# Three changes to a hybrid encoder block: weight splits moved between engines, left factors moved ahead, a projection's tile shape

## The chip, the cores and the metric

One core of a Trainium2 chip runs the whole layer. Its engines work side by side, each through its own queue in order: TensorE (PE; its weight loads are listed as PEld) multiplies, VectorE (DVE), ScalarE (ACT) and GpSimd (POOL) work element by element, SyncE (SP) issues the DMAs. The metric is the device time of one execution in microseconds. [...]

## The reference

One encoder layer on x of 512 x 1024 in float32, conditioned on a vector c:

```
mod = silu(c) @ w_ada + b_ada                     # sh1, sc1, g1, sh2, sc2, g2
u   = layer_norm(x) * (1 + sc1) + sh1
z   = u @ w_in                                    # q f i g u v ga gb, 1024 columns each
y_a = hgrn2_mixer(zq, zf, zi, zg) @ w_proj_a      # gated linear recurrence, chunks of 64
y_b = gmlp_mixer(zu, zv) @ w_proj_b               # gelu(u) * (W_s layer_norm(gelu(v)) + b)
mix = (sigmoid(zga + b0) * y_a + sigmoid(zgb + b1) * y_b) @ w_out
h   = layer_norm(alpha * x + g1 * mix) * ln1_w + ln1_b
u2  = layer_norm(h) * (1 + sc2) + sh2
a, b = split(u2 @ w_ffn_in);  ffn = (silu(a) * b) @ w_ffn_out
out = layer_norm(alpha * h + g2 * ffn) * ln2_w + ln2_b
```

## The kernel before, in words

Every float32 product is made of three fp32r matmuls: each operand is split into a rounded high part (ScalarE copies it to fp32r, L149 and L381) and the rest (a subtraction, mostly on VectorE, L150 and L382), and `mm3` (L216) adds high x high, high x low and low x high. So each block of weights, up to 1 MB, is loaded by SP into one of two `raw` buffers and split into one of two pairs `whi`, `wlo`, before TensorE may use it. `Block.split_part(k, n, eng)` (L138) splits n of a block's row groups, with the low part on the engine `eng`; `get()` (L203) hands out the next block and, one tick later, splits the block after it and loads the one after that. A tick is a mark in TensorE's order of work: `later(n, fn)` writes fn's instructions out n ticks on.

TensorE's and SP's order is that of the program. The other engines' order is made by a planner, which takes what it reckons ready, by program order or by a stated priority. Only in the lead stage (L423 to L511) are VectorE, ScalarE and GpSimd in the order written, too, and a few instructions elsewhere are pinned to it (`keep_in_program_order`, so the first two uq sums of `mixes`, L552).

The lead stage makes layer_norm(x) transposed and modulated (`uf`, split into `uh`, `ul`) one group k of 128 channels at a time, and multiplies it at once with the first 6 x 128 columns of `zu`, two k for each of four blocks of 256 x 768 weights (`lead`, 9 matmuls of 512 columns a half). The scale and shift of channels 2p, 2p+1 come from eight multiply-adds of VectorE over rows of w_ada (`step`, L342, 128x512) into `adaacc`, eight matmuls against ones (L361, the function `fin`), and an addition (L363). One turn p of the loop (L481) has in VectorE's order: steps 2 and 3 of the next pair of k, the low part `ul` of k+1, steps 4 to 7, then the additions after L361, steps 0 and 1 of the pair after, and `ul` of k+2. The next block's two row groups are split in the middle of the turn: high parts on ScalarE, low parts on GpSimd (L499, the engine `G`).

After it come the remaining two column groups of zu (`zw`, the plain columns, 48 matmuls), and then zv as a product in seven factors (`zt7`, L599: 24 matmuls each, with sums of weights for four of the factors, L191, and sums of left sides made by `mixes`, L542: four sums `uq` of high and low parts, four further sums and four splits, each 128x1024).

The output projection (w_out, scaled by `gate1` at L147 before its split) runs with tokens as the stationary side: `gemm_t` (L228) takes 128 tokens tt and one of four blocks of 1024 x 256 of w_out, 24 matmuls with 256 columns moving. The first block's products for tt 0 and 1 stand ahead (`head`, L1016). Each 128 x 512 half result is added to the residual (L1042) and put into statistics (L1043); then layer norm, a second one (`un`, L1030), a transposition on TensorE (L979), modulation and splits into `left` factors for the FFN's products (L1093), with weights `prod` split by L381 and L382.

Of the kernel before, what the change touches and what calls it, by code (L numbers as in the profile page):

```python
# [11 lines left out]
OP = mybir.AluOpType  # L12
# [38 lines left out]
def body(ctx, tc, x, c, w_ada, b_ada, w_in, b_gate, lb_logits, norm_w, w_proj_a, g_ln_w, g_ln_b,  # L51
# [52 lines left out]
    def tick():  # L104
        clock[0] += 1
        run_due()
# [109 lines left out]
    def mm3(ps, ah, al, bh, bl, start, stop):  # L216
        PE.matmul(ps, ah, bh, start=start, stop=False)  # L217
        PE.matmul(ps, ah, bl, start=False, stop=False)  # L218
        PE.matmul(ps, al, bh, start=False, stop=stop)  # L219
# [8 lines left out]
    def gemm_t(ps, w, tt, ah, al, k0=0, k1=KT):  # L228

        s = slice(tt * P, tt * P + P)  # L230
        for k in range(k0, k1):
            mm3(ps, ah[k][:, s], al[k][:, s], w[0][:, k, :], w[1][:, k, :], k == 0, k == KT - 1)
        if k1 == KT:
            tick()
# [19 lines left out]
    blocks += [Block([wcols(w_out, q * 256, 256)], gate=lambda q=q: gate1[:, q * 256:(q + 1) * 256], pool=(None if q == 1 else (lambda: (ub, ua)) if q == 3 else (lambda: (ub, ub)))) for q in range(4)]  # L254
# [168 lines left out]
    with tc.manual_schedule(engines={mybir.EngineType.DVE, mybir.EngineType.Activation, mybir.EngineType.Pool}):  # L423
# [57 lines left out]
        for p in range(KT // 2):  # L481
# [15 lines left out]
            if more:  # L497
                for kk in range(2):
                    nxt.split_part(kk, 1, G)  # L499
            else:  # L500
                nxt.split()
# [7 lines left out]
            if more:  # L509
                x_transpose(k + 3)  # L510
# [135 lines left out]

    zw(8 - NL, lambda j, ps: A.activation(gu[j], ps, AF.Gelu), j0=NL)
    later(5, gmlp_params)
    later(8, w_transpose)
    for fn in mixes(ua, True):  # L650
        fn()
# [364 lines left out]
    head = [acc_ps().rearrange("p (a b) -> p a b", a=2) for _ in range(2)]  # L1016
    for k in ((0, KT - 1), (KT - 1, KT)):
        for tt in range(2):
            gemm_t(head[tt][:, 0, :], wo[0], tt, mh, ml, *k)
# [12 lines left out]
    for tt in range(NT):  # L1032
        ht = h1t(tt)
        bst = sm.tile([P, 2, 6], F32, name="bst")
        for hf in range(2):
            first = hf == 0 and tt < 2
            ps = head[tt] if first else acc_ps().rearrange("p (a b) -> p a b", a=2)
            for i in range(first, 2):
                gemm_t(ps[:, i, :], wo[2 * hf + i], tt, mh, ml)
            with ahead_of_weights():  # L1040
                sl = slice(hf * 512, (hf + 1) * 512)
                V.scalar_tensor_tensor(ht[:, sl], ht[:, sl], ALPHA, ps.rearrange("p a b -> p (a b)"), op0=OP.mult, op1=OP.add)  # L1042
                V.bn_stats(bst[:, hf, :], ht[:, sl])  # L1043
# [241 lines left out]
```

## Time and profile before

| | us |
|---|---|
| median of three runs | 936.15 (934.73 to 936.59) |
| the profiled execution | 935.53 |
| its span, first to last instruction | 933.7 |
| TensorE busy | 899.9 (96%) |
| VectorE busy | 731.7 (78%) |
| ScalarE busy | 412.4 (44%) |
| GpSimd busy | 144.3 (15%) |
| mean granted clock | 0.993 |

Of 933.7 us TensorE is idle for 33.8. The page's slices show TensorE at nine tenths or more in nearly all of the 40 slices, so a gain can come from its idle time, or from doing its work in fewer or cheaper matmuls. A matmul's row gives its start and a modelled duration that overlaps the next one; the pace is the distance between starts. In a timeline, the bracket at the end of a row is the idle time of the engine just before it and what ended that.

### The profile page before, as it was taken

To read this page: it belongs to the slowest core of one execution; us is meant where nothing else is said; L and a number is where in the kernel's file an instruction comes from. 1 tells how busy PE (TensorE), PEld (TensorE's weight loads), DVE (VectorE), ACT (ScalarE), POOL (GpSimd) and SP (SyncE) were. 2 spreads that over 40 slices of the span, in tenths; PEclk is the share of its full clock that TensorE was granted. 3 is DMA by queue.
4 is the path that set the end of the run, shared out by engine and by line. 5 is a ranking of instruction groups with operands and counts; after the bars stand their busy time and mean duration, and the time that the engine had idled before them with its cause. 6 is when DMAs were issued, how large, how long until landed. Compare 5 with 4: busy or idle time off the path is not lost.

```text
span 933.7 us, 13131 instructions
## 1 busy us (share of the span) xinstructions
PE 899.9 (96%) x5357; PEld 794.2 (85%) x5357; DVE 731.7 (78%) x1036; ACT 412.4 (44%) x542; POOL 144.3 (15%) x99
## 2 busy tenths in 40 slices
PE   5899999999999999999999999999999999999995
PEld 4677778888788888888888999899999999888884
DVE  5858995897987788886389878987888888974337
ACT  4355543334466676764323327634444445531210
POOL 2310020200000000000000011006665544000001
PEclk9999999999999999999999999999999999999998
DMA  9844225442333331312297634022343221832312
GB/s 309 280 127 176 93 82 175 163 153 91 88 96 90 89 85 53 91 46 91 71 348 233 234 106 137 1 91 91 113 140 111 91 91 56 306 136 91 113 46 90
DMA packets 107822, 118.33 MB, mean 127 GB/s; under 512 B 3617, under 2 KB 89714, under 8 KB 107762
## 3 DMA queue, kind: packets, MB, share of 16 engines
q1 hardware_dynamic: 106592, 117.45, 39.0%
q8 instruction: 42, 0.69, 0.3%
q10 hardware_dynamic: 1170, 0.05, 0.1%
q14 instruction: 18, 0.15, 0.1%
HBM read 115.39 MB, written 2.10 MB: 126 GB/s over the span
## 4 chain that ended last, share of the span: by engine, by line
PE 81%; DVE 11%; DMA 2%; ACT 2%; issue 2%; POOL 1%; POOLq 0%; DVEq 0%; ACTq 0%; SPq 0%
PE acc L1093 15%; PE acc L219 15%; PE acc L217 15%; PE acc L218 15%; PE sps L1093 7%; PE acc L599 5%; DVE adaacc L342 2%; POOL rn L307 1%; PE sps L818 1%; PE sps L599 1%; DMA ada<-in_w_ada_dram 1%; DVE h L314 1%; PE sps L361 1%; PE sps L668 1%; PE sps L862 1%
## 5 line engine op out<-in xcount | busy, mean ns | idle before, releaser
L1093 PE MATMUL acc<-left,prod 128*128 128x256 f32 x1296 | 159.6, 283 | 0.4 <-DVE left L382 0.4
L1093 PEld LDWEIGHTS acc<-left,prod 128*128 128x128 f32 x1296 | 157.2, 192 | 0.6 <-DVE left L382 0.6
L149 ACT ACTIVATE whi<-raw 128x1024 fp32r<-128x1024 f32 (+2 forms) x92 | 90.7, 1016 | 136.9 <-PE acc L219 64.8
L150 DVE TENSOR_TENSOR wlo<-raw,whi 128x1024 fp32r<-128x1024 f32 (+2 forms) x85 | 99.9, 1191 | 45.2 <-ACT whi L149 39.9
L217 PE MATMUL acc<-uh,whi 128*128 128x512 f32 x336 | 134.7, 401 | 0.0
L219 PE MATMUL acc<-uh,wlo 128*128 128x512 f32 x336 | 131.4, 391 | 1.2 <-DVE wlo L150 1.2
L218 PE MATMUL acc<-ul,whi 128*128 128x512 f32 x336 | 131.0, 390 | 0.0
L219 PEld LDWEIGHTS acc<-uh,wlo 128*128 128x128 f32 x336 | 63.0, 188 | 15.2 <-DVE wlo L150 1.6
L1093 PE MATMUL sps<-left,prod 128*128 128x256 f32 x576 | 73.4, 283 | 2.0 <-DVE prod L382 2.0
L218 PEld LDWEIGHTS acc<-ul,whi 128*128 128x128 f32 x336 | 63.3, 188 | 12.0
L217 PEld LDWEIGHTS acc<-uh,whi 128*128 128x128 f32 x336 | 63.2, 188 | 11.7
L1093 PEld LDWEIGHTS sps<-left,prod 128*128 128x128 f32 x576 | 70.8, 192 | 2.4 <-DVE prod L382 2.4
L342 DVE SCALAR_TENSOR_TENSOR adaacc<-ada,cond,adaacc 128x512 f32<-128x512 f32 x82 | 70.4, 859 | 2.1 <-DMA ada<-in_w_ada_dram 0.6
L382 DVE TENSOR_TENSOR prod<-raw,prod 128x1024 fp32r<-128x1024 f32 x42 | 54.9, 1308 | 21.2 <-ACT prod L381 21.2
L307 POOL TENSOR_TENSOR rn<-rn,mhalf 128x1 f32<-128x1 f32 x16 | 18.5, 1158 | 339.6 <-DVE rn L306 339.6
L218 PE MATMUL acc<-wlo,hs 128*128 128x512 f32 x176 | 68.5, 389 | 0.0
L217 PE MATMUL acc<-whi,hs 128*128 128x512 f32 x176 | 68.5, 389 | 0.0
L219 PE MATMUL acc<-whi,hs 128*128 128x512 f32 x176 | 68.5, 389 | 0.0
L381 ACT ACTIVATE prod<-raw 128x1024 fp32r<-128x1024 f32 x42 | 44.4, 1058 | 41.2 <-PE acc L1093 21.4
L382 DVE TENSOR_TENSOR prod<-rawu,prod 128x1024 fp32r<-128x1024 f32 x22 | 47.7, 2169 | 8.3 <-ACT prod L381 7.8
L871 POOL TENSOR_TENSOR ss<-ss,mhalf 128x4 f32<-128x4 f32 x8 | 8.1, 1014 | 268.1 <-DVE ss L870 268.1
L217 PEld LDWEIGHTS acc<-whi,hs 128*128 128x128 f32 x176 | 33.0, 188 | 6.9
(293 smaller groups left out, 1854.0 us busy)
## 6 DMA issues: line engine op xcount, KB each, us to landing
ada<-in_w_ada_dram SPq DMA_DIRECT2D x32, 512.0 KB, 9.3
raw<-in_w_in_dram SPq DMA_DIRECT2D x13, 1024.0 KB, 5.7
raw<-in_w_in_dram SPq DMA_DIRECT2D x24, 512.0 KB, 5.4
raw<-in_w_ffn_in_dram SPq DMA_DIRECT2D x11, 1024.0 KB, 5.2
rawu<-in_w_ffn_in_dram SPq DMA_DIRECT2D x11, 1024.0 KB, 7.7
raw<-in_w_ffn_out_dram SPq DMA_DIRECT2D x10, 1024.0 KB, 5.1
ada<-in_w_ada_dram SPq DMA_DIRECT2D x8, 1024.0 KB, 7.8
rawq<-in_w_in_dram SPq DMA_DIRECT2D x4, 1024.0 KB, 7.9
```

The costliest lines, as they stand in the source:

```text
L149: A.activation(hi[:, k:k + n, :], self.raw[:, k:k + n, :], AF.Copy)
L150: eng.tensor_tensor(lo[:, k:k + n, :], self.raw[:, k:k + n, :], f32(hi[:, k:k + n, :]), OP.subtract)
L217: PE.matmul(ps, ah, bh, start=start, stop=False)
L218: PE.matmul(ps, ah, bl, start=False, stop=False)
L219: PE.matmul(ps, al, bh, start=False, stop=stop)
L307: G.tensor_tensor(rn[:, 0:1], rn[:, 0:1], mhalf[:, 0:1], OP.pow)
L314: V.scalar_tensor_tensor(xa, xa, rn[:, 0:1], wb[:, 1, :], op0=OP.mult, op1=OP.add)
L342: V.scalar_tensor_tensor(a, r, cond[:, k:k + 1], a, op0=OP.mult, op1=OP.add)
L381: A.activation(hi, src, AF.Copy)
L382: V.tensor_tensor(lo, src, f32(hi), OP.subtract)
L599: PE.matmul(o, a[:, k, s], b[:, k, :], start=n in (1, 5, 6) and k == 0 and a is ah and b is w[0], stop=n in (2, 4, 3) and k == 3 and a is ...
L1093: PE.matmul(ps[:, i, :], w[:, wi, k, cl], a[:, ai, k, :], start=first and st == (0, 0, 0, 0), stop=last and st == (1, 3, 0, 1), skip_group ...
```

## The change

The low part of the first row group of each next lead block is now made on VectorE behind steps 4 to 7, and the second row group is split at the end of the turn, behind `ul` of k+2, on VectorE too. `mixes(ua, True)` stands ahead of the plain columns. w_out is cut into four blocks of 512 x 512 in place of 1024 x 256 (rows q % 2, columns q // 2), `gemm_t` takes two of them for 24 matmuls with 512 columns moving, and ticks twice in it (before: once for each 24 matmuls of 256). `head` so makes the whole first half, 512 columns, for tt 0 and 1.

```diff
--- before.py
+++ after.py
@@ -229,9 +229,9 @@
 
         s = slice(tt * P, tt * P + P)
         for k in range(k0, k1):
-            mm3(ps, ah[k][:, s], al[k][:, s], w[0][:, k, :], w[1][:, k, :], k == 0, k == KT - 1)
-        if k1 == KT:
-            tick()
+            mm3(ps, ah[k][:, s], al[k][:, s], w[k // 4][0][:, k % 4, :], w[k // 4][1][:, k % 4, :], k == 0, k == KT - 1)
+            if k % 4 == 3:
+                tick()
 
     SEC = {n: i * D for i, n in enumerate(["q", "f", "i", "g", "u", "v", "ga", "gb"])}
     NL = 6
@@ -251,7 +251,9 @@
     blocks += [Block(fqg[2 * i:2 * i + 2]) for i in range(12)]
     blocks += [Block([wcols(w_in, SEC["ga"] + q * 256, 256)]) for q in range(4)]
     blocks += [Block([wcols(w_proj_a, q * 256, 256)]) for q in range(4)]
-    blocks += [Block([wcols(w_out, q * 256, 256)], gate=lambda q=q: gate1[:, q * 256:(q + 1) * 256], pool=(None if q == 1 else (lambda: (ub, ua)) if q == 3 else (lambda: (ub, ub)))) for q in range(4)]
+    blocks += [Block([w_out[q % 2 * 512:(q % 2 + 1) * 512, q // 2 * 512:(q // 2 + 1) * 512]], 4, 512,
+                     gate=lambda q=q: gate1[:, q // 2 * 512:(q // 2 + 1) * 512],
+                     pool=(None if q == 1 else (lambda: (ub, ua)) if q == 3 else (lambda: (ub, ub)))) for q in range(4)]
     KB = [(0, 4), (4, 4), (8, 4), (20, 2), (12, 4), (16, 4)]
 
 
@@ -495,8 +497,7 @@
             if more:
                 steps(p + 1, 4, 8)
             if more:
-                for kk in range(2):
-                    nxt.split_part(kk, 1, G)
+                nxt.split_part(0, 1)
             else:
                 nxt.split()
             lead(k + 1, w, 0)
@@ -507,6 +508,7 @@
                 modulate(k + 2)
             lead(k + 1, w, 1)
             if more:
+                nxt.split_part(1, 1)
                 x_transpose(k + 3)
         bpos[0] = KT // 2
     for j in range(NL):
@@ -644,11 +646,11 @@
             A.activation(gp["wT"][0:64, 4 * h:4 * h + 4, :], ps[0:64], AF.Copy)
             A.activation(gp["wT"][64:128, 4 * h:4 * h + 4, 64:128], ps[64:128, :, 64:128], AF.Copy)
 
+    for fn in mixes(ua, True):
+        fn()
     zw(8 - NL, lambda j, ps: A.activation(gu[j], ps, AF.Gelu), j0=NL)
     later(5, gmlp_params)
     later(8, w_transpose)
-    for fn in mixes(ua, True):
-        fn()
     gv = [ub.tile([P, 2, D], F32, name=f"gv{i}", tag="u") for i in range(2)]
     zt7(lambda tt: gv[tt // 2][:, tt % 2, :], AF.Gelu)
     for tt in (2, 3, 0, 1):
@@ -1013,10 +1015,10 @@
                 left_split(3, a12, ts)
 
 
-    head = [acc_ps().rearrange("p (a b) -> p a b", a=2) for _ in range(2)]
+    head = [acc_ps() for _ in range(2)]
     for k in ((0, KT - 1), (KT - 1, KT)):
         for tt in range(2):
-            gemm_t(head[tt][:, 0, :], wo[0], tt, mh, ml, *k)
+            gemm_t(head[tt], wo[0:2], tt, mh, ml, *k)
 
     mlag, nlag = [5, 5, 5, 9], [5, 5, 5, 3]
     rn2, uns = {}, {}
@@ -1034,12 +1036,12 @@
         bst = sm.tile([P, 2, 6], F32, name="bst")
         for hf in range(2):
             first = hf == 0 and tt < 2
-            ps = head[tt] if first else acc_ps().rearrange("p (a b) -> p a b", a=2)
-            for i in range(first, 2):
-                gemm_t(ps[:, i, :], wo[2 * hf + i], tt, mh, ml)
+            ps = head[tt] if first else acc_ps()
+            if not first:
+                gemm_t(ps, wo[2 * hf:2 * hf + 2], tt, mh, ml)
             with ahead_of_weights():
                 sl = slice(hf * 512, (hf + 1) * 512)
-                V.scalar_tensor_tensor(ht[:, sl], ht[:, sl], ALPHA, ps.rearrange("p a b -> p (a b)"), op0=OP.mult, op1=OP.add)
+                V.scalar_tensor_tensor(ht[:, sl], ht[:, sl], ALPHA, ps, op0=OP.mult, op1=OP.add)
                 V.bn_stats(bst[:, hf, :], ht[:, sl])
         with ahead_of_weights():
             mv, rn = ln_fin(bst)
```

## Rows read from the trace of the kernel before

**Rows 1.** Waits of TensorE, whole span: in total, times, the longest (us).

```profile
PE sps L361 <- DVE adaacc L342: 5.7, 3, 2.4
...
PE acc L599 <- DVE wlo L382: 2.1, 3, 1.6
PE sps L1093 <- DVE prod L382: 2.0, 2, 1.1
PE acc L219 <- DVE wlo L150: 1.2, 1, 1.2
PE sps L599 <- DVE wlo L382: 0.9, 1, 0.9
```

**Rows 2.** The chain that ended last, lead stage: start, us, what.

```profile
41.44 2.23 DVE adaacc L342
...
45.95 0.76 DVE adaacc L342
```

**Rows 3.** Timeline of GpSimd, lead stage: start, us, instruction, [idle before, releaser].

```profile
40.83 4.53 POOL L150 TENSOR_TENSOR wlo<-raw,whi 128x768 fp32r<-128x768 f32 x2 [8.21 <-ACT whi L149]
```

**Rows 4.** Timeline of VectorE, lead stage.

```profile
19.86 0.96 DVE L150 TENSOR_TENSOR wlo<-raw,whi 128x768 fp32r<-128x768 f32 x1 [0.54 <-ACT whi L149]
...
48.01 0.16 DVE L363 TENSOR_TENSOR mod<-sps,bmod 128x4 f32<-128x4 f32 x1 [1.31 <-PE sps L361]
...
49.69 0.69 DVE L412 TENSOR_TENSOR ul<-uf,uh 128x512 fp32r<-128x512 f32 x1 [0.32 <-ACT uh L411]
...
52.62 6.04 DVE L342 SCALAR_TENSOR_TENSOR adaacc<-ada,cond,adaacc 128x512 f32<-128x512 f32 x4
```

**Rows 5.** Timeline of ScalarE, lead stage.

```profile
39.92 1.56 ACT L149 ACTIVATE whi<-raw 128x768 fp32r<-128x768 f32 x2
```

**Rows 6.** Timeline of TensorE, lead stage.

```profile
33.32 1.44 PE L361 MATMUL sps<-ones,adaacc 128*128 128x128 f32 x8 [2.37 <-DVE adaacc L342]
...
46.85 1.13 PE L361 MATMUL sps<-ones,adaacc 128*128 128x128 f32 x8 [1.66 <-DVE adaacc L342]
...
58.80 1.13 PE L361 MATMUL sps<-ones,adaacc 128*128 128x128 f32 x8 [1.67 <-DVE adaacc L342]
...
70.49 0.39 PE L217 MATMUL acc<-uh,whi 128*128 128x512 f32 x1
```

**Rows 7.** Stretches: length, busy of PE PEld DVE ACT POOL (count), clock, DMA share, GB/s.

```profile
34.00:38.00 4.00, 4.00 (x15) 3.25 (x14) 2.82 (x6) 1.41 (x2) 0.00 (x0) 0.57 1.09 349
...
42.00:44.00 2.00, 2.00 (x10) 1.62 (x10) 1.97 (x2) 0.00 (x0) 2.00 (x2) 1.00 0.05 20
```

**Rows 8.** Timeline of VectorE from the plain columns to the third factor.

```profile
64.92 2.36 DVE L150 TENSOR_TENSOR wlo<-raw,whi 128x1024 fp32r<-128x1024 f32 x2 [0.26 <-ACT whi L149]
72.79 2.36 DVE L382 TENSOR_TENSOR wlo<-raw,whi 128x1024 fp32r<-128x1024 f32 x2 [5.51 <-ACT whi L381]
75.07 2.35 DVE L550 TENSOR_TENSOR uq<-uh,ul 128x1024 f32<-128x1024 f32 x2
...
90.04 1.22 DVE L382 TENSOR_TENSOR mix<-uq,mix 128x1024 fp32r<-128x1024 f32 x1
```

**Rows 9.** The chain, whole span: a run of 512-column matmuls, one of 256.

```profile
108.15 10.91 PE acc L599 x48
...
636.06 5.76 PE acc L1093 x48
```

**Rows 10.** Timeline of TensorE, first matmul of the output projection.

```profile
525.55 0.28 PE L217 MATMUL acc<-wu,mh 128*128 128x256 f32 x1
```

**Rows 11.** Timeline of VectorE, output projection.

```profile
536.84 1.21 DVE L150 TENSOR_TENSOR wu<-raw,wu 128x1024 fp32r<-128x1024 f32 x1
541.17 1.23 DVE L382 TENSOR_TENSOR prod<-raw,prod 128x1024 fp32r<-128x1024 f32 x1 [3.12 <-ACT prod L381]
...
545.87 0.69 DVE L1042 SCALAR_TENSOR_TENSOR h<-h,acc 128x512 f32<-128x512 f32 x1
...
550.00 0.68 DVE L1043 BATCH_NORM_STATS2 bst<-h 128x6 f32<-128x512 f32 x1
```


## The prediction

> **What bounds the kernel now.** I read the waits of TensorE first, since TensorE is busy for 96% of the span: its idle time in mid-kernel is short and stands in few places. The reader should see three of them [rows 1]: 5.7 us in three waits of L361 for VectorE's sums `adaacc` (lead stage), 3.0 us (2.1 and 0.9) of the factors' matmuls L599 for low parts, with 1.2 us more of L219 just behind them, and 2.0 us of the FFN's first products for `prod`. Everything else between is one dense row of matmuls, where only the price of a matmul counts. Then I read the chain and the engines' timelines at these places.
>
> In the lead stage the chain shows why VectorE is late: of the four steps of a turn two take 2.23 us (one stands for both), the fourth 0.76 [rows 2]. The slow two lie in the time in which GpSimd makes two low parts, 4.53 us from 40.83 [rows 3]; at 45.95 GpSimd is done and the step is quick again. It isn't the DMA: in 42 to 44 us its share is 0.05 while the steps crawl [rows 7]. So GpSimd beside VectorE costs 2 x (2.23 - 0.76) = 2.94 us a turn on the engine that TensorE waits for.
>
> **Part 1, lead splits.** Per turn GpSimd loses two subtractions; VectorE gets them, at 0.96 us for 128x768, 0.88 from start to next start [rows 4]. Take the turn from the addition at 48.01 to the end of step 7, 52.62 + 6.04 = 58.66: 10.65 us now [rows 4]. Less 2.94 is 7.71. The second row group's low part stands in it ahead of steps 2 and 3: 0.88, and up to 0.25 in which VectorE waits for ScalarE's high part of 0.78 us [rows 5], which queues behind `uh` and so ends after `ul` (49.69 + 0.69); behind that wait stand the steps. That makes 8.6 to 8.85 us. TensorE's own turn is from the end of one L361 (46.85 + 1.13 = 47.98) to the moment at which the next could start (58.80 - 1.67 = 57.13), 9.15 us [rows 6]. So VectorE comes in 0.2 to 0.5 us ahead of TensorE with the 0.14 us between them counted, and the three waits of 2.37, 1.66 and 1.67 us go (-5.7). What is late next is TensorE itself. The first row group's low part (0.88) falls behind step 7, into the 1.31 us in which VectorE waits for L361 [rows 4]: nothing, and if that cover were gone, 0.88 a turn. The moved ScalarE copies have their cover in ScalarE's share of 44%.
>
> [...] Behind the waits of 1.66 and 1.67 us L361 ran at 1.13, with no dip [rows 6]. With no wait I expect no dip: -1.9, bounds 0 and -1.9. I take -1.7 for it, since VectorE's margin is thin: part 1 is -7.4. Bounds: -7.6, and -4.2 if each turn keeps 0.5 us of waiting and the clock still dips. The data are there: DMA is done with its early burst before 42 us [rows 7], and by my turns the last pair's steps start at 42.4. The raw buffers come free 2 to 3 us later in each turn than by GpSimd, but turns are shorter by as much; SP's next loads behind them start at about the same time.
>
> **Part 2, mixes ahead.** VectorE ends the last lead split at 64.92 + 2.36, then waits 5.51 us for ScalarE's copy of factor 1 (72.79) and only then starts on `mixes` (75.07), which end at 90.04 + 1.22 [rows 8]. They are 12 instructions at 1.14 us from start to start, 13.7 us. They hold nothing that waits for the plain columns: `uh` and `ul` are complete before. Put ahead, they start behind the last split, 7.8 us sooner with respect to TensorE, and fill the hole. No DMA and no SP entry moves with them. VectorE's backlog, from which the 3.0 us of waits come [rows 1], is so paid off; I count -3.0. Of the 1.2 us at L219, behind layer-norm work on the same queue, I count half, -0.6. Against it: the low parts of factor 1 (2 x 1.14) now compete with `mixes`. In times less 7.4, VectorE starts at 67.3 - 7.4 = 59.9, so `mixes` end at 73.6 and, were factor 1 wholly behind, it would be split at 75.9. TensorE starts on the plain columns at 70.5 - 7.4 = 63.1 [rows 6] and wants factor 1 after 48 x 0.227 = 10.9 us, at 74.0, in halves: 0.4 us of waiting as value, 1.7 as bound, and nobody else stands behind that wait but TensorE. Part 2: -3.2, bounds -4.2 and +1.7.
>
> **Part 3, 512 columns.** A run of 48 matmuls takes 10.91 us at 512 columns and 5.76 at 256: 227 and 120 ns each [rows 9]. The projection's 384 of 256 become 192 of 512: 384 x 0.120 = 46.1, 192 x 0.227 = 43.6, so 2.5 us less on TensorE. [...] But TensorE isn't late there: it waits 2.0 us for `prod` afterwards [rows 1], and VectorE's chain through residuals, layer norms and splits is the later one. So the saving passes only as far as that chain moves. `head` now ends at 525.55 + 10.9 = 536.4 [rows 10], with the first half of tt 1 in it, which before came after six runs of 24 matmuls, at 525.55 + 17.3 = 542.8. VectorE is idle for 3.12 us before 541.17 [rows 11], and tt 1's L1042 and L1043 (545.87 and 550.00, some 1.3 us together) fit into that hole. That advances the chain behind by 1.3 us. The other way, tt 0's second half is done at 536.4 + 5.5 = 541.9, where it was 525.55 + 5 x 2.88 = 539.95; VectorE came to it at 542.3 only, behind the split at 541.17, so this costs nothing, and up to 1.9 us if the planner puts it ahead of that split. Scaling by gate1 and the splits keep their sizes (128x1024), and so the weights keep their loads (1 MB each). Part 3: -1.3, bounds -2.5 and +1.9.
>
> **Sum.** -7.4 - 3.2 - 1.3 = -11.9: a span of 921.8, and with the 1.8 us between span and time of the profiled run (935.53 - 933.7) 923.6. The median lies 0.6 above the profiled run: 924.3.
>
> **Rivals.** (a) The waits move on instead of going. Between the parts VectorE's order is the planner's, and `mixes` may take factor 1's place in the queue; lead turns may keep 0.5 us each and the clock its dip. Then -4.2, -1 and -0.5: 930.4. For it: VectorE's margin of 0.2 to 0.5 us, and its work at 8 to 9 tenths. Against it: the turn's sum, from rows of the same turn.
>
> (b) The edit doesn't do what it says: the planner leaves `mixes` where they were, as far as VectorE goes, and part 3 stays hidden. Only the lead stage, whose order is written out, changes: -7.4, 928.8. For it: nothing forces the sums after the first two. Against it: those two are pinned, and VectorE has nothing else to do at that place.
>
> (c) Slower: the steps don't crawl because of GpSimd but for some other cause in these 4 us, and stay at 2.23. Then each turn gets 0.88 + 0.25 more on the chain, 3.4 in three, another dip of the clock 1.9, and if parts 2 and 3 bring nothing 941.5. It decides from the point at which a slow step keeps more than 2.23 - 0.56 = 1.67 us (two steps then save less than the 1.13 added). Against it: slow and quick steps of one turn differ in nothing but GpSimd's work, and the DMA is idle [rows 3, 7]. [...]
>
> **How the numbers follow.** Forecast 0.62, (a) 0.2, (b) 0.12, (c) 0.03, others 0.03. The likeliest case runs from about 920 (all bounds but the last microseconds) to 927; (a) and (b) reach 930.4, so 919.5 to 930.5 holds 8 in 10. 0.2%, about what a measurement here can tell from no change, is 1.9 us: faster 0.93, same 0.03, slower 0.04.
>
> **What would show it.** Right: steps L342 at 0.75 us throughout the lead stage, GpSimd with one low part there in place of seven, L361 without waits, a granted clock near 1.0 in 30 to 40 us, the plain columns from about 63 us; `uq` on VectorE ahead of factor 1's low parts, no L599 waits; in the output projection starts of matmuls 227 ns apart, and waits of L1093 for `prod` longer than 2.0 us by some 1.2. Wrong: steps still over 1.67 us, waits of L361 of over 0.5 us a turn, or a wait of over 2 us at the first factor.

## The result, and the profile after

| | before | after |
|---|---|---|
| median, beside one another | 936.37 us (4 runs) | 921.87 us (921.51 to 922.03, 4 runs) |
| the profiled execution | 935.53 | 921.51 |
| its span | 933.7 | 919.7 |
| TensorE busy | 899.9 | 894.5 |
| VectorE busy | 731.7 | 727.4 |
| GpSimd busy | 144.3 | 132.3 |

The changed kernel is faster: a ratio of 0.9847, 95% interval 0.9830 to 0.9865. The forecast was 924.3 us (919.5 to 930.5). A second set of four runs gave 921.42 us (921.36 to 921.55). In the changed kernel the lines lie two further on: L342 is now L344, L361 L363, L382 L384, L599 L601, L1042 L1044 and L1093 L1095.

The waits of TensorE after (in total, times, the longest, in us) answer to [rows 1]:

```profile
PE acc L219 <- DVE wlo L150: 1.2, 1, 1.2
PE acc L1095 <- DVE left L384: 1.0, 1, 1.0
...
PE sps L1095 <- DVE prod L384: 0.5, 1, 0.5
PE acc L1095 <- ACT left L383: 0.4, 1, 0.4
PE acc L601 <- DVE wlo L384: 0.3, 1, 0.3
PE sps L363 <- DVE adaacc L344: 0.2, 1, 0.2
```

Of the 5.7 us of L361 for `adaacc` 0.2 are left; of the 3.0 us of L599, 0.3. Those 0.3 are not factor 1's: they stand in a second product in seven factors, that of zi, at 238.86, where the kernel before has the same wait at 250.87 (0.33 us in both), a place that the change does not touch. The 1.2 us of L219 stand untouched.

**Lead stage.** VectorE after, answering to [rows 4] (start, us, instruction, [idle before, releaser]):

```profile
36.84 3.11 DVE L344 SCALAR_TENSOR_TENSOR adaacc<-ada,cond,adaacc 128x512 f32<-128x512 f32 x4
39.87 0.95 DVE L150 TENSOR_TENSOR wlo<-raw,whi 128x768 fp32r<-128x768 f32 x1
41.55 0.16 DVE L365 TENSOR_TENSOR mod<-sps,bmod 128x4 f32<-128x4 f32 x1 [0.74 <-PE sps L363]
```

The four steps take 3.11 us instead of 6.04, and the low part behind them lies in the time in which VectorE would wait for L363 anyhow. TensorE after, answering to [rows 6]:

```profile
30.34 1.13 PE L363 MATMUL sps<-ones,adaacc 128*128 128x128 f32 x8 [0.18 <-DVE adaacc L344]
...
40.47 1.05 PE L363 MATMUL sps<-ones,adaacc 128*128 128x128 f32 x8
...
50.49 1.05 PE L363 MATMUL sps<-ones,adaacc 128*128 128x128 f32 x8
```

The margin can be read from these two views: the sums of the second turn end at 36.84 + 3.11 = 39.95, and L363 starts at 40.47, so VectorE is 0.5 us ahead. The stretch that answers to [rows 7] (length, busy PE PEld DVE ACT POOL, clock, DMA share, GB/s) has the granted clock at 1.00 (full speed), where it was 0.57:

```profile
34.00:38.00 4.00, 4.00 (x21) 3.26 (x21) 3.93 (x6) 2.26 (x3) 0.00 (x0) 1.00 1.09 350
```

**Factors.** VectorE after, answering to [rows 8]:

```profile
56.51 2.36 DVE L150 TENSOR_TENSOR wlo<-raw,whi 128x1024 fp32r<-128x1024 f32 x2 [0.26 <-ACT whi L149]
58.79 2.35 DVE L552 TENSOR_TENSOR uq<-uh,ul 128x1024 f32<-128x1024 f32 x2
...
67.79 1.22 DVE L384 TENSOR_TENSOR wlo<-raw,whi 128x1024 fp32r<-128x1024 f32 x1
...
73.47 1.22 DVE L384 TENSOR_TENSOR wlo<-raw,whi 128x1024 fp32r<-128x1024 f32 x1
75.02 1.23 DVE L384 TENSOR_TENSOR mix<-uq,mix 128x1024 fp32r<-128x1024 f32 x1 [0.34 <-ACT mix L383]
```

`uq` follows the last lead split without a gap, and the hole of 5.51 us is filled. The two halves of factor 1 are taken in between the mixes, at 67.79 and 73.47.

**Output projection.** VectorE after, answering to [rows 11]:

```profile
524.85 1.28 DVE L1044 SCALAR_TENSOR_TENSOR h<-h,acc 128x512 f32<-128x512 f32 x2
...
527.78 1.22 DVE L384 TENSOR_TENSOR prod<-raw,prod 128x1024 fp32r<-128x1024 f32 x1 [1.05 <-ACT prod L383]
530.06 0.69 DVE L1044 SCALAR_TENSOR_TENSOR h<-h,acc 128x512 f32<-128x512 f32 x1 [1.06 <-PE acc L219]
...
547.28 0.69 DVE L1044 SCALAR_TENSOR_TENSOR h<-h,acc 128x512 f32<-128x512 f32 x1 [0.56 <-PE acc L219]
...
578.07 1.22 DVE L1063 TENSOR_TENSOR t<-raw,rawu 128x1024 f32<-128x1024 f32 x1
```

Two additions of first halves (tt 0 and tt 1) stand together at 524.85, and the hole of 3.12 us ahead of the first `prod` has shrunk to 1.05. But there are two waits now that were not there before, for a result of TensorE (1.06 at 530.06 and 0.56 at 547.28). TensorE's first matmul of the projection, answering to [rows 10]:

```profile
513.54 0.39 PE L217 MATMUL acc<-wu,mh 128*128 128x512 f32 x1
```

**Where the time went.** I put each matmul's start before beside its start after. The difference, in us:

| at (start before -> after) | earlier by | what lies between |
|---|---|---|
| 22 to 25 us | 0.8 | start of the kernel, ahead of the change |
| first L361, 33.32 -> 30.34 | 3.0 | first wait |
| second L361, 46.85 -> 40.47 | 6.4 | second wait and the clock |
| third L361, 58.80 -> 50.49 | 8.3 | third wait |
| plain columns, 70.49 -> 62.08 | 8.4 | |
| 102.09 -> 90.06, behind the last wait of the factors | 12.0 | waits of the factors |
| projection, 525.55 -> 513.54 | 12.0 | nothing, for 423 us |
| last wait, 595.72 -> 581.69 | 14.0 | projection |

So: start 0.8 (the first matmul of the lead stage, ahead of the edits in TensorE's and VectorE's order, starts between 21.82 and 24.18 us in the 13 traces of this document, so this is none of the change's doing), lead 7.6, factors 3.6, projection 2.0.

### The profile page after: what moved, and what is told of

It reads as the page before. It is cut to its first block, busy times and chain, and to the rows that moved or that the text cites. A ratio compares the mean times of both kernels' runs of the same rounds, so it can differ in the third digit from the quotient of the medians.

```text
span 919.7 us, 12746 instructions
## 1 busy us (share of the span) xinstructions
PE 894.5 (97%) x5165; PEld 782.7 (85%) x5165; DVE 727.4 (79%) x1042; ACT 412.1 (45%) x542; POOL 132.3 (14%) x93
## 4 chain that ended last, share of the span: by engine, by line
PE 83%; DVE 10%; DMA 2%; POOL 2%; ACT 1%; issue 1%; POOLq 0%; DVEq 0%; ACTq 0%; SPq 0%
PE acc L1095 16%; PE acc L219 15%; PE acc L217 15%; PE acc L218 15%; PE sps L1095 7%; PE acc L601 5%; PE sps L601 2%; POOL rn L309 2%; PE sps L820 1%; DMA ada<-in_w_ada_dram 1%; PE sps L363 1%; DVE h L316 1%; PE sps L864 1%; PE sps L670 1%; PE sps L855 1%
## 5 line engine op out<-in xcount | busy, mean ns | idle before, releaser
L1095 PE MATMUL acc<-left,prod 128*128 128x256 f32 x1296 | 159.9, 283 | 1.4 <-DVE left L384 1.0
L1095 PEld LDWEIGHTS acc<-left,prod 128*128 128x128 f32 x1296 | 157.3, 192 | 1.9 <-DVE left L384 1.2
L150 DVE TENSOR_TENSOR wlo<-raw,whi 128x1024 fp32r<-128x1024 f32 (+2 forms) x91 | 105.5, 1174 | 45.3 <-ACT whi L149 39.9
L219 PE MATMUL acc<-uh,wlo 128*128 128x512 f32 x336 | 131.4, 391 | 1.2 <-DVE wlo L150 1.2
L219 PEld LDWEIGHTS acc<-uh,wlo 128*128 128x128 f32 x336 | 63.1, 188 | 15.1 <-DVE wlo L150 1.6
L1095 PE MATMUL sps<-left,prod 128*128 128x256 f32 x576 | 73.3, 283 | 0.5 <-DVE prod L384 0.5
L1095 PEld LDWEIGHTS sps<-left,prod 128*128 128x128 f32 x576 | 70.9, 192 | 0.7 <-DVE prod L384 0.7
L384 DVE TENSOR_TENSOR prod<-raw,prod 128x1024 fp32r<-128x1024 f32 x42 | 55.0, 1308 | 19.2 <-ACT prod L383 19.1
L219 PE MATMUL acc<-whi,hs 128*128 128x512 f32 x176 | 68.5, 389 | 0.0
L344 DVE SCALAR_TENSOR_TENSOR adaacc<-ada,cond,adaacc 128x512 f32<-128x512 f32 x82 | 61.5, 750 | 2.3 <-DMA ada<-in_w_ada_dram 0.7
L384 DVE TENSOR_TENSOR prod<-rawu,prod 128x1024 fp32r<-128x1024 f32 x22 | 47.8, 2171 | 8.3 <-ACT prod L383 7.7
L219 PEld LDWEIGHTS acc<-whi,hs 128*128 128x128 f32 x176 | 33.0, 188 | 7.0
```

The lines of the kernel that those rows point to most:

```text
L150: eng.tensor_tensor(lo[:, k:k + n, :], self.raw[:, k:k + n, :], f32(hi[:, k:k + n, :]), OP.subtract)
L344: V.scalar_tensor_tensor(a, r, cond[:, k:k + 1], a, op0=OP.mult, op1=OP.add)
L384: V.tensor_tensor(lo, src, f32(hi), OP.subtract)
L1095: PE.matmul(ps[:, i, :], w[:, wi, k, cl], a[:, ai, k, :], start=first and st == (0, 0, 0, 0), stop=last and st == (1, 3, 0, 1), skip_group ...
```

## The experiments

The base in the text is the changed kernel (921.87, and 921.42 where it ran beside the others) or the kernel before; the kernel before gave medians of 935.6 to 935.8 us beside these runs.

### One part at a time

Part 1 alone on the kernel before:

```diff
-                for kk in range(2):
-                    nxt.split_part(kk, 1, G)
+                nxt.split_part(0, 1)
...
             lead(k + 1, w, 1)
             if more:
+                nxt.split_part(1, 1)
                 x_transpose(k + 3)
```

> The kernel before with part 1 alone (both low parts of the lead blocks on VectorE, the second at the end of the turn). If GpSimd's two subtractions are what stretches the sums, the three waits of L361 (5.7 us) and the dip of the clock go, some 7.5 us less, 928 to 929.5 us; and if the stretch of 3 us behind the lead stage stays as it was, the waits of L599 are still 3 us. If the sums are slow for another cause (rival c), they stay at 2.23 us and the time is 936 or more. If part 1 also pays off VectorE's later backlog, so that part 2 has little of its own, it is under 927.

Measured: 926.64 us (926.22 to 927.08), 0.9907 of before (0.9885 to 0.9929): 9.0 us less by the medians, more than the 928 to 929.5 us that I expected. In the two traces TensorE's starts move by 8.0 us over the lead stage (0.28 ahead at its start, 8.32 at its end). The mean granted clock differs too: 0.997 in three of these four runs, and 0.990 to 0.993 in 15 of the 21 of the kernel before; how much of the last microsecond is the clock's was not measured. Its waits of TensorE:

```profile
PE acc L599 <- DVE wlo L382: 2.1, 3, 1.6
PE sps L1093 <- DVE prod L382: 1.9, 2, 1.1
PE acc L219 <- DVE wlo L150: 1.2, 1, 1.2
PE sps L599 <- DVE wlo L382: 0.9, 1, 0.9
```

All three waits of L361 are gone, and those of the other places are what they were in [rows 1]: nothing that part 1 gains is lost behind it, and none of it comes from elsewhere. So the branch "under 927", into which the time falls, does not hold: part 1 paid off nothing of what part 2 takes.

Part 2 alone:

```diff
+    for fn in mixes(ua, True):
+        fn()
     zw(8 - NL, lambda j, ps: A.activation(gu[j], ps, AF.Gelu), j0=NL)
     later(5, gmlp_params)
     later(8, w_transpose)
-    for fn in mixes(ua, True):
-        fn()
```

> The kernel before with part 2 alone (mixes written ahead of the plain columns). If the hole of 5.5 us on VectorE is what the sums fill, the waits of L599 fall from 3.0 us to under 0.5 and the time by 3 to 3.6 us, to 932.5 to 933.5. If the planner leaves VectorE's order as it was (rival b), no change: 936. If factor 1's low parts now come late, a wait of up to 1.7 us at the first factor and 934 to 935.

Measured: 932.13 us (930.72 to 933.20), 0.9967 (0.9953 to 0.9981), 3.5 us less, and 3.6 by the traces. In its waits L599 has 0.3 us left of 3.0 (those of zi), and L219 its whole 1.2.

Part 3 alone (the lines on w_out, `gemm_t` and `head` of the diff, nothing else):

```diff
-            gemm_t(head[tt][:, 0, :], wo[0], tt, mh, ml, *k)
+            gemm_t(head[tt], wo[0:2], tt, mh, ml, *k)
...
-            for i in range(first, 2):
-                gemm_t(ps[:, i, :], wo[2 * hf + i], tt, mh, ml)
+            if not first:
+                gemm_t(ps, wo[2 * hf:2 * hf + 2], tt, mh, ml)
```

> The kernel before with part 3 alone (512 columns moving in the output projection). If VectorE's chain lets through only what tt 1's early half fills, 1.3 us less (935); if the whole of TensorE's 2.5 us passes, 934; in the changed kernel the matmuls behind the projection start 2.1 us earlier with respect to those ahead of it, so 934.3 is what the parts add up to if they don't touch one another.

Measured: 933.40 us (932.61 to 934.38), 0.9979 (0.9967 to 0.9991), 2.2 us less, and by the traces 2.2 too: more than the order's 1.3, less than TensorE's whole 2.5. The three parts alone add up to 9.0 + 3.5 + 2.2 = 14.7 us; together they bring 14.5 beside the first runs of before and 14.4 beside the last. By the traces, without the differences at the start, it is 8.0 + 3.6 + 2.2 = 13.8 us alone and 13.2 together. They take little from one another.

### Order or pace: what in part 3 pays

The changed kernel with the old blocks of 256 columns, but in the new order (both quarters of a first half for tt 0 and 1 ahead). TensorE does the matmuls of before here.

```diff
     for k in ((0, KT - 1), (KT - 1, KT)):
         for tt in range(2):
             gemm_t(head[tt][:, 0, :], wo[0], tt, mh, ml, *k)
+    for tt in range(2):
+        gemm_t(head[tt][:, 1, :], wo[1], tt, mh, ml)
...
-            for i in range(first, 2):
+            for i in range(0 if not first else 2, 2):
                 gemm_t(ps[:, i, :], wo[2 * hf + i], tt, mh, ml)
```

> The changed kernel with w_out in four blocks of 1024 x 256 again and 256 columns moving, but the head in the new order: both quarters of the first half for tt 0 and 1 ahead. So it has part 3's order without its pace. If part 3 works by the order (tt 1's first half in VectorE's hole), it is as fast as the changed kernel, 922, with longer busy TensorE and shorter waits of L1093. If it works by the pace of the matmuls, it loses 2 us: 924.

Measured: 922.40 us (921.92 to 923.54), 0.9863 (0.9841 to 0.9886). That is 0.5 us above the changed kernel's first set and 1.0 above its second. By the traces the projection starts 0.3 us earlier than in the changed kernel (513.25 and 513.54), the first L1095 stands 2.2 us later (561.06 and 558.85) and the last wait 0.8 later (582.46 and 581.69): the pace saves 2.5 us of TensorE's time, as forecast, and 1.1 of them are left behind the last wait. Of part 3's 2.0 to 2.2 us some 0.9 to 1.7 are order, 0.5 to 1.1 pace. (VectorE's order among its additions and splits differs a little between the two kernels as well, so the parting is not exact.) VectorE of this kernel shows how pace can count at all:

```profile
530.72 0.69 DVE L1044 SCALAR_TENSOR_TENSOR h<-h,acc 128x512 f32<-128x512 f32 x1 [0.68 <-PE acc L219]
...
548.87 0.69 DVE L1044 SCALAR_TENSOR_TENSOR h<-h,acc 128x512 f32<-128x512 f32 x1 [1.63 <-PE acc L219]
```

At 548.87 VectorE waits 1.63 us for a result of TensorE; with 512 columns it waits 0.56 us, at 547.28. At the earlier place it is the other way round, 0.68 and 1.06 us; together 2.31 and 1.62. VectorE's chain has places where it is TensorE that is late.

### GpSimd beside VectorE: reading, writing, or only more work

Rival (c) said that the steps are slow for some other reason than GpSimd. In each of these kernels work is added to the changed one that nobody reads: it goes to a scratch tile, and the layer's own work is left whole.

```diff
+        scr = ub.tile([P, 2, D], F32, name="scr", tag="u")
+        V.memset(scr, 0.0)
...
                 nxt.split_part(0, 1)
+                for i in range(2):
+                    G.tensor_tensor(scr[:, i, 0:768], scr[:, i, 0:768], f32(nxt.hl[0][:, 0, :]), OP.subtract)
```

> The changed kernel, and in each of the first three lead turns two more subtractions of 128x768 on GpSimd, on a scratch tile and the block's first high part, let go when that is made, as in the kernel before; nobody waits for them. If GpSimd's reading beside VectorE is what stretched the sums, two steps of a turn take 2.2 us again, less the 0.4 us by which VectorE is early: waits of L363 of some 2.5 us in three turns and perhaps the dip of the clock, 929 to 931.5. If the stretch had another cause (rival c: the data, the order), the sums stay at 0.76 and the time at 922.

Measured: 934.62 us (932.99 to 935.02), 0.9985 (0.9974 to 0.9995): the whole gain of the lead stage is gone, and more. GpSimd, and VectorE's four steps of the same turn:

```profile
43.08 4.46 POOL L504 TENSOR_TENSOR scr<-scr,whi 128x768 f32<-128x768 f32 x2 [9.83 <-ACT whi L149]
```

```profile
42.84 6.03 DVE L344 SCALAR_TENSOR_TENSOR adaacc<-ada,cond,adaacc 128x512 f32<-128x512 f32 x4
```

The second kernel has GpSimd as busy at the same place, but writing only (two memsets; the small copy makes them wait for the high part as the subtractions do):

```diff
                 nxt.split_part(0, 1)
+                G.tensor_copy(scr[:, 0, 0:4], f32(nxt.hl[0][:, 0, 0:4]))
+                for i in range(2):
+                    G.memset(scr, 0.0)
```

> The same, but GpSimd fills the scratch tile twice (128x2048, memset) behind a copy of four columns that waits for the high part: it writes and reads next to nothing. If the two engines exclude each other by what they read, the sums stay at 0.76 us: 922. If it is any work of GpSimd in SBUF that stops VectorE, the steps stretch as with the subtractions, by the length of the fills.

Measured: 924.19 us (923.20 to 925.10), 0.9873 (0.9858 to 0.9888). GpSimd and VectorE:

```profile
38.94 3.68 POOL L505 MEMSET scr<- 128x2048 f32 x2
```

```profile
38.75 3.11 DVE L344 SCALAR_TENSOR_TENSOR adaacc<-ada,cond,adaacc 128x512 f32<-128x512 f32 x4
```

Beside 3.68 us of writing the four steps take 3.11 us, as with no GpSimd at all; beside 4.46 us of reading, 6.03. So in these kernels it is not that GpSimd is busy, but that it reads. (The subtraction reads two tiles. An operation of GpSimd that reads only one was not run.)

Both kernels have a flaw that I had not thought of: the scratch tile is filled on VectorE ahead of the first turn (1.76 us and 0.38 us of idling), which delays that turn by about 2 us. In the second kernel's trace the lead stage is thereby 2.5 us longer than in the changed one's:

```profile
32.24 1.13 PE L363 MATMUL sps<-ones,adaacc 128*128 128x128 f32 x8 [2.71 <-DVE adaacc L344]
```

One wait in the first turn; at 42.35 and 52.39 us L363 starts without any. Against this kernel as base the reading costs 934.62 - 924.19 = 10.4 us. To have it without the flaw I filled the tile on GpSimd:

```diff
-        V.memset(scr, 0.0)
+        G.memset(scr, 0.0)
```

> The changed kernel with two 128x768 subtractions a turn added on GpSimd, which read a scratch tile and the high part of the lead's weight and write to the scratch (nobody reads it). Unlike the first such run, the scratch is filled on GpSimd ahead of the loop, so that VectorE has nothing new in its queue. Theory (GpSimd's reading operations take turns with VectorE's two-operand ones): two of the four steps of each group of sums beside them take about 2.2 instead of 0.76 us, so a group takes about 6 instead of 3.1; less the margin of 0.2 to 0.5 us that VectorE has in a turn, TensorE waits about 2.5 us at L363 in each of the three turns, and with the clock that falls behind such waits (0 to 2 us) the time is 929 to 931.5. Rival (what slowed the first such run was the fill on VectorE and what followed from it): groups of sums of 3.1 us, no waits, 922.

Measured: 932.19 us (931.19 to 932.44), 0.9962 (0.9949 to 0.9975), beside 921.42 for the changed kernel: 10.8 us, and above the 929 to 931.5 that I expected. GpSimd of the second turn, then VectorE's steps of that turn one by one, as the chain that ended last has them (start, us, what), then TensorE:

```profile
41.06 4.53 POOL L504 TENSOR_TENSOR scr<-scr,whi 128x768 f32<-128x768 f32 x2 [9.07 <-ACT whi L149]
```

```profile
40.98 0.67 DVE adaacc L344
41.68 2.23 DVE adaacc L344
43.93 2.22 DVE adaacc L344
46.18 0.76 DVE adaacc L344
```

```profile
33.48 2.05 PE L363 MATMUL sps<-ones,adaacc 128*128 128x128 f32 x8 [3.97 <-DVE adaacc L344]
...
47.08 1.13 PE L363 MATMUL sps<-ones,adaacc 128*128 128x128 f32 x8 [1.75 <-DVE adaacc L344]
...
59.88 1.28 PE L363 MATMUL sps<-ones,adaacc 128*128 128x128 f32 x8 [2.52 <-DVE adaacc L344]
```

The steps behave as in the kernel before, 2.23 and 2.22 beside GpSimd and 0.76 behind it ([rows 2, 3] there), the waits are back, 8.2 us in all, and the clock falls at the first and the third of them (0.93 and 0.65 in 30 to 38 us, 0.84 and 0.73 in 58 to 66, so 3.4 us lost). Together that is 11.6 us; by the traces the lead stage is 12.3 us longer than in the second profiled execution of the changed kernel, which began it 0.9 us later. The expectation was too low at two places: in the first turn VectorE has no margin to begin with (0.18 us of waiting in the changed kernel, and 0.7 with 256 columns in the new order and with the layer norm later), so its wait is 3.97 us and not 2.5, and the clock fell twice. Rival (c) is out: the steps are slow where GpSimd reads (2.23 and 2.22 us beside its subtractions), and quick where it writes (3.11 us for four) or rests (0.76).

The third kernel of this group puts more work on VectorE instead, to measure how much it could still take:

```diff
             if more:
                 nxt.split_part(1, 1)
+                for i in range(2):
+                    V.tensor_tensor(scr[:, i, 0:768], scr[:, i, 0:768], f32(nxt.hl[0][:, 1, :]), OP.subtract)
                 x_transpose(k + 3)
```

> The changed kernel with two more subtractions of 128x768 on VectorE at the end of each of the first three turns, 1.76 us more a turn; nobody reads them. VectorE is early by some 0.4 us in turns 1 and 2, so L363 should wait 1.3 to 1.4 us in each of the two turns that follow such an end: 2.7 us, 924.6. If VectorE's margin were larger than its rows say, under 923.5. The waits are shorter than the 2.37 us behind which the clock fell: with a dip behind them 926 or more.

Measured: 927.26 us (925.75 to 929.16), 0.9901 (0.9884 to 0.9917), with the same fill on VectorE in it, so 3.1 us above the kernel with the memsets. TensorE at the first and the third L363:

```profile
33.24 2.05 PE L363 MATMUL sps<-ones,adaacc 128*128 128x128 f32 x8 [2.67 <-DVE adaacc L344]
...
57.67 1.13 PE L363 MATMUL sps<-ones,adaacc 128*128 128x128 f32 x8 [1.21 <-DVE adaacc L344]
```

The first is the fill's. In the third turn 1.74 us of added work (two subtractions, 0.87 us each from start to start) give 1.21 us of waiting: a margin of 0.53 us, as the two views of the changed kernel say. In the second turn there is no wait, as TensorE itself runs at a lower clock (0.50 in 34 to 38 us). So one wait came where I expected two. The time is in the branch that I gave for a dip of the clock (926 or more), and the trace has one: in the profiled execution, 929.16 us, 3.4 us are lost in 30 to 42 us (0.82, 0.50, 0.82). The fill, which I had not counted, adds its delay to that.

### One low part a turn back on GpSimd

```diff
-                nxt.split_part(1, 1)
+                nxt.split_part(1, 1, G)
```

> The changed kernel with the low part of the second row group of each lead weight made on GpSimd again (1 of the 2 low parts a turn, at the same place in the program, behind the sums). Theory (it is the overlap of GpSimd's reading with the sums that costs, one step at a time): the subtraction starts when its weights' high part is there and lies beside VectorE's sums or beside nothing; at most one or two of the four steps are stretched by 1.4 us each, VectorE is spared 0.9 to 1.1 us, so TensorE waits 0 to 1.7 us a turn at L363: 922 to 927. Rival (any low part on GpSimd costs what the two did, since the queue's order does not keep it off the sums): waits above 2 us in each turn and 928 or more. Rival (the amount of work on VectorE is what counts): none, and 921.9 or a little below.

Measured: 922.03 us (920.97 to 922.85), 0.9856 (0.9839 to 0.9872): no difference from 921.42 that these runs can show. TensorE has no wait at L363 for `adaacc`. GpSimd and VectorE of the second turn:

```profile
34.43 2.28 POOL L150 TENSOR_TENSOR wlo<-raw,whi 128x768 fp32r<-128x768 f32 x1 [11.66 <-ACT whi L149]
```

```profile
34.26 3.00 DVE L344 SCALAR_TENSOR_TENSOR adaacc<-ada,cond,adaacc 128x512 f32<-128x512 f32 x2
37.79 3.10 DVE L344 SCALAR_TENSOR_TENSOR adaacc<-ada,cond,adaacc 128x512 f32<-128x512 f32 x4
```

The two steps beside it take 3.00 us instead of 1.53: one of the two is stretched, by 1.47 us. VectorE is spared a subtraction of 0.88 us, so it loses 0.6 us in the turn, about its whole margin, and TensorE does not notice. What costs is not a low part on GpSimd as such: it is each step that is stretched beside one (2.22 us for the one at 35.04, 0.75 for the one at 34.26), and two a turn were more than the margin bears.

### The 1.2 us that stayed, and a faster kernel

In the changed kernel VectorE takes the split for the gate block's matmuls (L219) at 123.74, behind layer norms:

```profile
123.14 0.68 DVE L660 BATCH_NORM_STATS2 bst<-gv 128x6 f32<-128x512 f32 x1
123.74 1.20 DVE L150 TENSOR_TENSOR wlo<-raw,whi 128x1024 fp32r<-128x1024 f32 x1
```

Here the layer norm of gelu(v) is written out two ticks on, behind that block's split; the work is the same.

```diff
-    for tt in (2, 3, 0, 1):
-        va = gv[tt // 2][:, tt % 2, :]
...
+    def gv_norm():
+        for tt in (2, 3, 0, 1):
+            va = gv[tt // 2][:, tt % 2, :]
...
+    later(2, gv_norm)
```

> The changed kernel with the layer norm of gelu(v) written out two ticks into the next plain columns, behind the split of the second gate block. The wait of 1.2 us of L219 is still there in the changed kernel; if its cause is that this split stands behind the layer norm in VectorE's queue, the wait goes and the time falls to 920.7. If the split waits for ScalarE or a buffer, no change: 921.9. If the layer norm comes too late for the spatial matmuls, new waits, over 922.

Measured: **919.45 us** (918.88 to 920.39), 0.9824 (0.9809 to 0.9838), faster than both kernels. VectorE now takes both halves of a split at once, ahead of the statistics:

```profile
113.52 2.36 DVE L150 TENSOR_TENSOR wlo<-raw,whi 128x1024 fp32r<-128x1024 f32 x2
115.79 1.29 DVE L661 BATCH_NORM_STATS2 bst<-gv 128x6 f32<-128x512 f32 x2
```

The wait of L219 is gone from the list. TensorE's starts, 0.95 us ahead of the changed kernel's in the lead stage, are 2.35 ahead at 125 us and 2.6 at the end: 1.4 come at that place, where the wait was 1.2; the 0.95 stand ahead of the edit and belong to this one execution, whose mean granted clock is 0.996, where the changed kernel's profiled execution has 0.995, with 0.63 and 0.95 in 18 to 26 us. By the medians it is 2.0 to 2.4 us, so by some 0.5 to 1 us more than I can place. The wait went with the order in VectorE's queue; moving `mixes` had left it at 1.2 us.

### The changed kernel once more

> The changed kernel once more, beside the next two kernels and the kernel before, as the base for both and for the layer norm that was moved. If its times spread as little as in its first runs (921.5 to 922.0 us), 921.9 within 0.5, no waits of TensorE at L363, and the clock near 1.0 from 26 us to the end of the lead. If its first runs were lucky in the clock, some of these runs lie 2 to 6 us higher.

Measured: 921.42 us (921.36 to 921.55, four runs), 0.9851 (0.9836 to 0.9866). The kernel before ran from 931.25 to 937.39 in 21 runs of one set; the changed one stays within 0.7 us over both of its sets.

## Why the prediction was right, point by point

**What bounds.** The three places of waiting were the right ones: but for 0.8 us at the start, the starts of the matmuls move there and nowhere else, and they keep their distance for the 423 us between the factors and the projection.

**Part 1: -7.4 forecast, -7.6 in the pair of traces, -8.0 alone.** Each step of the working holds. The steps went from 2.23 to 0.76 us, two of four a turn; the split behind the sums lies in VectorE's wait for L363; the margin of 0.2 to 0.5 us is 0.50 by two views and 0.53 by added work. Of the 5.7 us of waits 5.5 went. What was left over is the first turn's 0.18 us, in which I had put the margin of the later turns. The clock took 1.7: between the first and the second L361 TensorE gains 3.40 us, 1.66 of them the wait, so 1.74 is left for the clock (0.57 in 34 to 38 us before, 1.00 after) and what comes with it, where I took 1.7. The 0.4 us above 5.5 + 1.7 lie in the first matmuls behind a wait (the third turn is 1.93 us shorter, its wait was 1.67). No run shows the 1.7 us (1.9 in the bounds and in rival (c)) as what a wait of TensorE costs in clock; what the runs showed in its place is 0.43 x 4 = 1.7 us in the one profiled execution of before, and 0 to 3.4 us behind the first waits of over 2 us in seven kernels (last section); that the sum fits the medians as well is in part luck. (That GpSimd's reading stretches the steps and its writing does not, the pair of 6.03 us beside 4.46 of subtractions and 3.11 beside 3.68 of memsets shows.)

**Part 2: -3.2 forecast, -3.6 measured in the traces, -3.5 by the medians.** The sum is nearly right with two terms off in opposite directions, which is luck. Half of L219's 1.2 us was counted to it, and nothing of it went: the step "of the 1.2 us at L219, behind layer-norm work on the same queue, I count half" failed, since VectorE's backlog was not what put that split late; its place in the queue was. And the waits that went were worth more than the list says. Of its 3.0 us, 0.33 stand in the product of zi and stayed; but where starts before lie over 0.3 us apart, they lie 4.0 us in all beyond the pace of 0.227 (60 to 112 us), with part 2 alone 0.5. A wait is the idle time of the engine; the first matmuls behind it (90.18 to 90.52 in the kernel before, 0.34 us to the next start and not 0.23) cost as well. The wait of factor 1 was forecast at 0.4 us; it is 0.04 in its row and costs 0.3 in starts (74.32 to 75.08 for two).

**Part 3: -1.3 forecast, -2.0 to -2.2 measured.** The direction was right, the size not. Read at VectorE's `t`, an instruction that stands at the same place in both orders, VectorE's chain moves from 592.10 to 578.07, 14.0 us; less the 12.0 with which the projection begins, it advances by 2.0 where I forecast 1.3. With the order alone it advances by 0.95 (its `t` at 578.85, its projection from 513.25), so order brings somewhat less than the 1.3, and pace, which I had put at nothing, another 1.1. The statement that failed is "TensorE isn't late there". It is late for VectorE at single results (530.06 and 547.28), and so part of the pace counted. On TensorE's side the 384 matmuls of 256 columns take 46.2 us and the 192 of 512 take 43.7; of these 2.5 us, and of 0.5 us less waiting behind them, 0.65 are given back in the 32 transpositions (L979), which lie 3.16 us before and 3.81 after, and 0.4 in the first products between the waits. The row of before that answers to the 578.07 of after, VectorE in the kernel before:

```profile
592.10 1.22 DVE L1061 TENSOR_TENSOR t<-raw,rawu 128x1024 f32<-128x1024 f32 x1
```

**What would show it.** Seen as written: steps at 0.75 us, one low part on GpSimd (1.84 us at 20.22), the clock at 1.00 in 30 to 40 us, the plain columns at 62.08 us, `uq` ahead of factor 1's low parts, and in the projection two distances between starts in 0.45 us (timeline of TensorE):

```profile
553.41 0.39 PE L217 MATMUL acc<-wu,mh 128*128 128x512 f32 x1
...
553.86 0.39 PE L219 MATMUL acc<-wu,ml 128*128 128x512 f32 x1
```

Not seen: L361 and L599 wholly without waits (0.18 us in the first turn, and 0.04 at factor 1), and the longer waits for `prod`. They fell from 2.0 to 0.5 us, with 1.0 for `left` new beside them. I had let TensorE come 2.5 us sooner and VectorE 1.3, so 1.2 more of waiting for the same thing; but VectorE came 2.0 sooner at the end, and the wait changed its object. The two sums, 2.4 before with the 0.4 for `left` and 1.9 after, say that TensorE lost nothing to a longer wait.

**Rivals.** (a) fell with the margin that held in the second and the third turn, and left 0.18 us in the first; (b) with `uq` at 58.79 and part 3 worth 2.2 us alone; (c) with the kernels in which GpSimd reads, writes, or does neither.

**The sum.** -7.6 - 3.6 - 2.0 and -0.8 of the start, which is none of the change's: 14.0 us of span, against -11.9 forecast. Without the start it is 13.2 us, 1.3 more than forecast, about half of it part 3. The forecast of 924.3 us lies 2.4 above the measured 921.87 by these 1.3, the 0.8, and a median 0.36 above the profiled execution where I took 0.6.

## What to carry to other kernels

A split on an idle engine was not free here: beside GpSimd's subtractions two of VectorE's four steps took 2.23 us instead of 0.76. Look at the mean time of the same instruction inside and outside of the other engine's rows, before moving work to where there is room. When a wait for an engine is to be explained, look at what stands ahead of the awaited instruction in that engine's queue and not only at how busy it is; one deferral of work that nobody needed yet was worth 1.4 us where its wait had been, the change of a matmul's shape 2.0 to 2.2. And an engine that is "not late" at its own waits can still be what another engine's chain waits for: both directions have to be read.

## What the runs showed of the hardware

**The times fit turns better than an even slowdown.** They look like two engines that take turns. Two subtractions of GpSimd did not stretch VectorE's four steps evenly. In the kernel with the clean fill the step that starts at 41.68 ends with the first subtraction (41.06 and half of 4.53, so 43.3) and its own 0.6 us or so; the next subtraction and the step at 43.93 do the same; the fourth takes its 0.76. Beside a single subtraction one step of two is long (0.75 and 2.22 us, 3.00 for both). And a subtraction that took 1.84 us beside no step (at 54.93 in the kernel with one low part on GpSimd) took 2.22 to 2.28 beside the steps, so each is longer beside the other. I had thought of it as one engine slowing the other down.

**The lower clock comes with some waits, not with all of like length.** First waits of TensorE at L361 or L363 in the profiled execution of each kernel that has one over 2 us, the granted clock in three stretches, and what it cost (4 us times what is missing to 1.00, summed):

| kernel | wait, us | 30 to 34 | 34 to 38 | 38 to 42 | lost, us |
|---|---|---|---|---|---|
| before | 2.37 | 1.00 | 0.57 | 1.00 | 1.7 |
| more work on VectorE | 2.67 | 0.82 | 0.50 | 0.82 | 3.4 |
| writing on GpSimd | 2.71 | 1.00 | 1.00 | 1.00 | 0 |
| part 2 alone | 3.00 | 0.76 | 0.81 | 1.00 | 1.7 |
| part 3 alone | 3.14 | 0.79 | 0.50 | 0.86 | 3.4 |
| reading on GpSimd, clean fill | 3.97 | 0.93 | 0.65 | 1.00 | 1.7 |
| reading on GpSimd, fill on VectorE | 4.59 | 0.87 | 0.50 | 0.78 | 3.4 |

In six of the seven the clock fell (to 0.50 to 0.81 over 34 to 38 us; in the kernel before it is 0.50 in each half microsecond from 34.0 to 37.0, 0.59 in the next and 1.00 behind that); in the one with a wait of 2.71 us it did not, though behind 2.37 and 2.67 us it did. Later waits differ in the same way: the third, 2.52 us with the clean fill and 2.51 with the fill on VectorE, has a dip in the one (0.84 and 0.73 in 58 to 66 us, matmuls of 512 columns 0.43 us apart from 61.38 to 63.52) and none in the other (0.23 us apart from 63.02 to 63.95). The rows of the stretch from 34 to 38 us, first with more work on VectorE, then with writing on GpSimd:

```profile
34.00:38.00 4.00, 4.00 (x14) 3.40 (x13) 2.29 (x5) 2.14 (x3) 0.00 (x0) 0.50 1.09 352
```

```profile
34.00:38.00 4.00, 4.00 (x22) 3.29 (x21) 3.59 (x5) 3.79 (x6) 0.00 (x0) 1.00 1.09 349
```

With writing on GpSimd, the clock had been at 1.00 from 18 us on, with more work on VectorE at 0.62 in 18 to 22 us; but the clean fill had 1.00 there too and dipped later. What decides it stays open: the wait alone doesn't. (At the start of the kernel the clock differs as well: over the same code it is 0.57 in 18 to 22 us with part 2 alone and 1.00 with writing on GpSimd.) The changed kernel has no such wait, and in both its profiled executions a clock of 1.00 from 26 to 62 us; its runs lie 0.7 us apart, where those of before spread over 6. The mean granted clock on record with each run says the same of one kernel. Of 41 runs of the kernel before, the four at 0.997 took 931.25 to 933.16 us and the 18 at 0.992 took 935.59 to 937.39. With writing on GpSimd, two runs at 0.996 and 0.997 took 923.2 and 923.3 us, two at 0.993 took 925.1; the trace is of the first kind. So in these runs the spread goes with the clock, and what part 1 wins back of it is no fixed sum; which dips the runs without a trace had was not seen.
